# Feed-forward blocks of a two-layer encoder in seven products for eight, in a hand-written order

## The chip, the core and the metric

One core of a Trainium2 chip runs the whole program. The metric is the device time of one execution in microseconds. Engines: PE (TensorE) multiplies, DVE (VectorE), ACT (ScalarE) and POOL (GpSimd) work elementwise, SP issues the transfers.

## The reference, cut to what matters

1024 tokens of 1024 features go through two layers. Each adds a mixer's output and then that of a feed-forward block (SwiGLU with 2816 hidden features) to the residual h; the change is in the second.

```python
u = rms_norm(h, g_ffn[layer])
h = h + swiglu(u, w_gate[layer], w_up[layer], w_down[layer])

def swiglu(u, w_gate, w_up, w_down):
    return (jax.nn.silu(u @ w_gate) * (u @ w_up)) @ w_down
```

The inputs are float32. A product is made as three matmuls of fp32r operands: each operand x is split into a rounded part hi and a rest lo = x - hi, and hi*hi + hi*lo + lo*hi is summed in PSUM (`mm3`, lines 158 to 162).

## The kernel before

Activations stand transposed: features on the 128 partitions, tokens in two halves (hf 0 and 1) of 512 columns. h is 8 x 2 tiles of 128x512.

Order of work: mixer 0 (`mixer0`), feed-forward 0, mixer 1 (`mixer1`), feed-forward 1. A mixer ends in its output projection (`out_half`, lines 296 to 312), 8 tiles of 24 matmuls for each half; the first half's is woven into the attention, the second half's stands alone. There each new tile of h goes through `feed` (lines 205 to 213): times the gain, split, squared and summed. The normalisation itself (`rstd`, lines 191 to 203: a matmul with ones, Ln and Exp on ACT, three instructions on DVE) is put on the products' results later.

The feed-forward (`ffn`, lines 314 to 363) goes by chunks of the 22 hidden tiles (`CHUNKS`). For each hidden tile it loads 128x1024 of w_gate and w_up, splits them (`weight`, lines 146 to 156: hi on ACT, lo on POOL), makes four results of 8 x 3 matmuls each, and then: times r (DVE, 331), Silu (ACT, 332), times r (POOL, 333), times the second result (DVE, 336), split (ACT and DVE). After a chunk, its part of w_down is multiplied and added to h (`add`, lines 344 to 348). The last chunk also feeds what comes next: `to_mixer1` (line 954) in layer 0, `to_out` and `finish` in layer 1.

A scheduler orders each engine's instructions from the program's order and their dependences. PSUM has two banks "mm", two pairs "z" and two banks "o". The heap "u" has 60 tiles of 128x512. All transfers go through SP's queue, which issues in order.

Of the kernel before, what the change touches and what calls it, by code (L numbers as in the profile page):

```python
# [9 lines left out]
F32 = mybir.dt.float32  # L10
# [10 lines left out]
CHUNKS = [[(0, 6), (6, 6), (12, 5), (17, 5)], [(0, 6), (6, 6), (12, 6), (18, 4)]]  # L21
# [12 lines left out]
FFN_TEMPS = {"h": (18, 512), "w": (3, 1024)}  # L34


class Stream:


    def __init__(self):  # L40
        self.h = [[], []]
        self.u = [([], []), ([], [])]
        self.acc = [None, None]
        self.r = [None, None]
        self.rc = [None, None]


class Trunk:
    def __init__(self, ctx, tc, a):
        self.tc, self.nc, self.a = tc, tc.nc, a  # L50
        self.n = 0
        pool = lambda name, bufs, **k: ctx.enter_context(tc.tile_pool(name=name, bufs=bufs, **k))
        self.cp = pool("consts", 1)
        self.wp = pool("weights", 1)
        self.hp = pool("heap", HEAP)
        self.lp = pool("loads", LOADS)
        self.sp = pool("small", 4)
        self.ps = pool("psum", 1, space=bass.MemoryType.PSUM)
        self.dp = pool("spill", 1, space=bass.MemoryType.DRAM)
        self.turn = self.wturn = 0  # L60
        self.pending = []
# [34 lines left out]
    def any_banks(self):  # L96
        self.turn += 1
        if self.turn % 3 == 0:
            return [self.out_bank(), self.out_bank()]
        t = self.banks()  # L100
        return [t[:, 0, :], t[:, 1, :]]

# [24 lines left out]


# [16 lines left out]

    def weight(self, src, n=1024, eng_hi="act", eng_lo="pool", into=None):
        self.wturn = (self.wturn + 1) % 3
        if "w" in self.temps and self.wturn == 0:
            raw, *parts = (self.tmp("w", dt, (P, 1024)) for dt in (F32, F32R, F32R)[:1 if into else 3])
        else:  # L150
            raw, *parts = (self.wp.tile([P, 1024], dt, tag=t, bufs=2, name=self.nm(t))
                           for t, dt in (("wr", F32), ("wh", F32R), ("wl", F32R))[:1 if into else 3])
        hi, lo = into or parts
        self.nc.sync.dma_start(raw[:, :n], src)
        self.split(raw[:, :n], hi[:, :n], lo[:, :n], eng_hi, eng_lo)
        return hi, lo

    def mm3(self, out, wh, wl, xh, xl, first, last):
        mm = self.nc.tensor.matmul
        mm(out, wh, xh, start=first, stop=False)  # L160
        mm(out, wh, xl, start=False, stop=False)  # L161
        mm(out, wl, xh, start=False, stop=last)  # L162

    def dense(self, out, w, x, ks, m=P):
        wh, wl = w
        for i, k in enumerate(ks):
            self.mm3(out, wh[:, k * m:(k + 1) * m], wl[:, k * m:(k + 1) * m], x[0][k], x[1][k],
                     i == 0, i == len(ks) - 1)
            yield 3 * MM_US
# [59 lines left out]

    def start(self, vts, proj):  # L230
# [8 lines left out]
        def token_values(hf, k):  # L239
            n = 8 * hf + k  # L240
            self.feed(s, hf, self.load(a["x"][hf, k]) if n else x0, G_MIX0 + k, "pool")
            if n < 2:
                qk[n] = self.weight(a["w_qkb"][n], eng_hi=("act", "dve")[n], eng_lo="dve",
                                    into=[self.tmp("a", F32R, (P, 1024)) for _ in range(2)])
# [4 lines left out]
            wh, wl = vw[k // 4]  # L249
            ks = slice(k % 4 * 256, k % 4 * 256 + 256)  # L250
            for r in range(4):
                ts = slice(r * P, (r + 1) * P)
                self.mm3(psv[hf][:, r // 2, r % 2 * 256:r % 2 * 256 + 256], s.u[hf][0][k][:, ts],
                         s.u[hf][1][k][:, ts], wh[:, ks], wl[:, ks], k == 0 and r % 2 == 0, k == KD - 1 and r % 2 == 1)

        def query_key(hf, k):
            if k == 0:
                psq[hf] = [self.bank(), self.bank()]
            ks = slice(k * P, (k + 1) * P)
            for i in range(2):  # L260
                self.mm3(psq[hf][i], qk[i][0][:, ks], qk[i][1][:, ks], s.u[hf][0][k], s.u[hf][1][k],
                         k == 0, k == KD - 1)
# [33 lines left out]
    def out_half(self, hf, w, parts, resid, goff, ks, s):  # L296

        nc = self.nc
        o = [x[0] for x in parts], [x[1] for x in parts]
        ahead = []  # L300
        for m in range(KD):
# [3 lines left out]
            wt = self.weight(w[m])  # L305
            ps = self.bank()
            yield from self.dense(ps, wt, o, ks)
            nc.vector.tensor_tensor(h, ps, x, ALU.add)
            s.h[hf].append(h)
            self.feed(s, hf, h, goff + m)  # L310
        if hf == 0:
            self.close(s, hf)

    def ffn(self, layer, s, parts, hold, done):

        nc, a = self.nc, self.a
        hs = s.h
        self.wturn = 0
        for ci, (f0, nf) in enumerate(CHUNKS[layer]):
            h1 = [([], []), ([], [])]  # L320
            for f in range(f0, f0 + nf):
                ws = [self.weight(a[n][layer, f]) for n in ("w_gate", "w_up")]
                ps = [self.any_banks(), self.any_banks()]
                sils = {}
                for hf, i in ((0, 0), (0, 1), (1, 0), (1, 1)) if f == 0 else ((0, 0), (1, 0), (0, 1), (1, 1)):
                    self.now(self.dense(ps[i][hf], ws[i], s.u[hf], range(KD)))
                    if s.r[1] is None:
                        self.close(s, 1)
                    if i == 0:
                        t = sils[hf] = self.unit()  # L330
                        nc.vector.tensor_tensor(t, ps[0][hf], s.r[hf], ALU.mult)  # L331
                        nc.scalar.activation(t, t, AF.Silu)  # L332
                        nc.gpsimd.tensor_tensor(t, t, s.r[hf], ALU.mult)  # L333
                        continue
                    t = sils[hf]
                    nc.vector.tensor_tensor(t, t, ps[1][hf], ALU.mult)  # L336
                    hi = self.unit(F32R) if f - f0 < nf - 3 else self.tmp("h", F32R)
                    lo = self.tmp("h", F32R)
                    self.split(t, hi, lo, "act", "dve")
                    h1[hf][0].append(hi)  # L340
                    h1[hf][1].append(lo)
            wsrc = lambda m: a["w_down"][layer, m, :, f0 * P:(f0 + nf) * P]

            def add(w, hf, m, cs=slice(0, HALF)):
                ps = self.bank()[:, 0:cs.stop - cs.start]
                x = [t[:, cs] for t in h1[hf][0]], [t[:, cs] for t in h1[hf][1]]
                self.now(self.dense(ps, w, x, range(nf)))
                nc.vector.tensor_tensor(hs[hf][m][:, cs], ps, hs[hf][m][:, cs], ALU.add)  # L348

            if ci < len(CHUNKS[layer]) - 1:  # L350
                for m in range(KD):
                    w = self.weight(wsrc(m), nf * P)
                    for hf in range(2):
                        add(w, hf, m)
                continue
            self.use_exp_ln()
            held = []
            for n, (hf, cs) in enumerate(parts):
                for m in range(KD):
                    while hold and len(held) < min(m + 3, KD):  # L360
                        held.append(self.weight(wsrc(len(held)), nf * P, into=[self.unit(F32R), self.unit(F32R)]))
                    add(held[m] if hold else self.weight(wsrc(m), nf * P), hf, m, cs)
                    done(n, m)
# [37 lines left out]
    def values(self, wsrc, s, kper, nk, ng, vts, hfs):  # L401
# [6 lines left out]
        for b0 in range(4 * hfs[0], 4 * hfs[-1] + 4, per):  # L408
            ps = self.bank()
            for b in range(per):  # L410
                hf, r = divmod(b0 + b, 4)
                ts = slice(r * P, (r + 1) * P)
                for k in range(nk):
                    wh, wl = ws[k // kper]
                    ks = slice((k % kper) * ncol, (k % kper + 1) * ncol)
                    self.mm3(ps[:, b * ncol:(b + 1) * ncol], u[hf][0][k][:, ts], u[hf][1][k][:, ts],
                             wh[:, ks], wl[:, ks], k == 0, k == nk - 1)
# [419 lines left out]
    def mixer0(self):  # L837
# [4 lines left out]
        half = lambda hf: self.out_half(hf, a["w_out0"], o_p[hf], lambda hf, m: a["x"][hf, m], G_FFN0, ks, out)  # L842
        with self.phase("mix0", MIX0_TEMPS):
# [53 lines left out]
            self.now(half(1))  # L897
        return out

    def mixer1(self, u, h_d):  # L900
# [3 lines left out]
        half = lambda hf: self.out_half(hf, a["w_out1"], o_p[hf], lambda hf, m: h_d[hf][m], G_FFN1,  # L904
                                        list(range(KD)), out)
        with self.phase("band", BAND_TEMPS):
# [37 lines left out]
            self.now(half(1))  # L944
        return out

    def run(self):
        nc, a = self.nc, self.a
        self.use_exp_ln()
        s = self.mixer0()  # L950
        h_d = self.spill("h_")
        nxt = Stream()

        def to_mixer1(hf, m):
            h = s.h[hf][m]
            self.feed(nxt, hf, h, G_MIX1 + m)
            nc.sync.dma_start(h_d[hf][m], h)
            if m == KD - 1:
                self.close(nxt, hf, columns=True)

        with self.phase("ffn0", FFN_TEMPS):
            self.ffn(0, s, [(hf, slice(0, HALF)) for hf in range(2)], False, to_mixer1)
        s = self.mixer1(nxt, h_d)
# [26 lines left out]
        with self.phase("ffn1", FFN_TEMPS):  # L990
            self.ffn(1, s, parts, True, to_out)
# [17 lines left out]
def _layout(i):  # L1009
# [40 lines left out]
    out["w_down"] = np.stack([_mtiles(i["w_down"][l]) for l in range(2)])  # L1050
# [38 lines left out]
```

## Time and profile before

| | |
|---|---|
| median of 3 runs | 2765.8 us (2762.65 to 2766.0) |
| the profiled execution | 2765.65 us |
| its span, first to last instruction | 2763.9 us |
| granted TensorE clock, mean | 0.994 |
| first feed-forward stage, about | 700 to 1410 us of the span |
| second feed-forward stage, about | 2010 us to the end |

In the profile a slice is a fortieth of the span (69 us), and each digit a busy share in tenths. A row of the timeline gives start, duration, engine, line, operation, out<-in, and in brackets how long the engine stood idle before it, and for whom. In a row of windows each engine has its busy microseconds and (x instructions). Matmul durations overlap (0.39 us each), so their spacing counts.

### The profile page before, as it was taken

Reading aid. Unit: us, or ns where it says so; the run is one execution under the profiler, and the core shown is the slowest. Engines: PE = TensorE matmul, PEld = TensorE weight load, DVE = VectorE, ACT = ScalarE, POOL = GpSimd, SP = SyncE. Lnnn points to the kernel's source line nnn. Section 1 sums busy time; section 2 is a strip of 40 time slices with the busy share of each in tenths; the row PEclk is TensorE's granted clock in tenths of the full one; section 3 lists DMA queues with packets and bytes.
Section 4 is the critical chain, followed back from the end, with each engine's and each line's share of the span. In section 5 each row is a group of like instructions: output and inputs, shape, how many; then the busy total and the mean of one; then the engine's idle time right before and its main releaser. Section 6 shows DMA issues by size and latency. Waiting matters only on the chain.

```text
span 2763.9 us, 31577 instructions
## 1 busy us (share of the span) xinstructions
PE 2694.1 (97%) x12502; PEld 2075.4 (75%) x12502; DVE 1359.1 (49%) x1899; ACT 936.0 (34%) x1419; POOL 967.4 (35%) x697
## 2 busy tenths in 40 slices
PE   7999989999999999999999999999999999999997
PEld 6766755567888888888887777766788888888886
DVE  6889787776321221222356666678742122122125
ACT  4766675454211111211243333334421111111114
POOL 3333225664332322323322334334433233233233
PEclk9999999999999999999999999999999999999999
DMA  4222100134111111111142222223411111111111
GB/s 134 54 62 65 37 15 24 45 115 130 59 39 56 49 39 57 40 52 54 50 147 68 80 69 80 79 73 109 149 62 38 54 54 37 56 51 38 58 39 69
DMA packets 69827, 178.49 MB, mean 65 GB/s; under 512 B 8368, under 2 KB 12336, under 8 KB 69680
## 3 DMA queue, kind: packets, MB, share of 16 engines
q1 hardware_dynamic: 69680, 176.48, 20.3%
q8 instruction: 98, 1.61, 0.2%
q14 instruction: 49, 0.40, 0.0%
HBM read 150.23 MB, written 15.73 MB: 60 GB/s over the span
## 4 chain that ended last, share of the span: by engine, by line
PE 80%; DVE 5%; issue 1%; ACT 1%; POOL 0%; DVEq 0%; ACTq 0%; POOLq 0%
PE mm L160 11%; PE mm L161 11%; PE mm L162 11%; PE z L160 8%; PE z L161 8%; PE z L162 8%; PE o L161 4%; PE o L162 4%; PE o L160 4%; PE o L435 4%; PE z L805 2%; PE z L779 1%; PE z L806 1%; PE z L724 1%; DVE f L697 1%
## 5 line engine op out<-in xcount | busy, mean ns | idle before, releaser
L140 POOL TENSOR_TENSOR wl<-wr,wh 128x1024 fp32r<-128x1024 f32 (+4 forms) x165 | 348.7, 2113 | 745.5 <-ACT wh L135 693.2
L160 PE MATMUL mm<-u,wh 128*128 128x512 f32 x970 | 389.3, 402 | 3.7 <-DVE u L137 2.0
L162 PE MATMUL mm<-u,wl 128*128 128x512 f32 x970 | 380.0, 392 | 0.1
L135 ACT CAST wh<-wr 128x1024 fp32r<-128x1024 f32 (+4 forms) x175 | 164.7, 941 | 598.2 <-PE mm L161 278.4
L161 PE MATMUL mm<-u,wh 128*128 128x512 f32 x768 | 301.7, 393 | 0.0
L160 PE MATMUL z<-u,wh 128*128 128x512 f32 x672 | 266.3, 398 | 0.0
L161 PE MATMUL z<-u,wh 128*128 128x512 f32 x672 | 262.5, 391 | 0.0
L162 PE MATMUL z<-u,wl 128*128 128x512 f32 x672 | 261.7, 389 | 0.0
L348 DVE TENSOR_TENSOR u<-mm,u 128x512 f32<-128x512 f32 (+1 forms) x136 | 89.6, 659 | 311.9 <-PE mm L162 311.4
L160 PEld LDWEIGHTS mm<-u,wh 128*128 128x128 f32 x970 | 182.4, 188 | 75.7 <-issue 32.9
L162 PEld LDWEIGHTS mm<-u,wl 128*128 128x128 f32 x970 | 182.3, 188 | 40.4 <-issue 2.9
L140 POOL TENSOR_TENSOR w<-w,w 128x1024 fp32r<-128x1024 f32 (+2 forms) x50 | 105.7, 2115 | 260.2 <-ACT w L135 260.2
L435 PE MATMUL o<-a,u 128*64 128x512 f32 (+3 forms) x768 | 174.1, 483 | 0.2 <-ACT a L808 0.2
L333 POOL TENSOR_TENSOR u<-u,u 128x512 f32<-128x512 f32 x88 | 114.5, 1302 | 159.5 <-ACT u L332 159.5
L336 DVE TENSOR_TENSOR u<-u,z 128x512 f32<-128x512 f32 x60 | 41.3, 689 | 262.3 <-PE z L162 223.1
L161 PEld LDWEIGHTS mm<-u,wh 128*128 128x128 f32 x768 | 144.7, 188 | 29.4 <-issue 4.6
L161 PE MATMUL mm<-h,wh 128*128 128x512 f32 x424 | 166.2, 392 | 0.0
L160 PEld LDWEIGHTS z<-u,wh 128*128 128x128 f32 x672 | 126.1, 188 | 39.2 <-DVE u L336 7.0
L676 POOL TENSOR_TENSOR b<-b,a 128x512 f32<-128x512 f32 (+3 forms) x80 | 108.1, 1352 | 117.0 <-ACT a L808 101.1
L162 PEld LDWEIGHTS z<-u,wl 128*128 128x128 f32 x672 | 126.2, 188 | 27.1
L331 DVE TENSOR_TENSOR u<-z,u 128x512 f32<-128x512 f32 x58 | 40.1, 692 | 214.4 <-PE z L162 214.4
L161 PEld LDWEIGHTS z<-u,wh 128*128 128x128 f32 x672 | 126.2, 188 | 25.5 <-issue 0.5
(225 smaller groups left out, 5990.5 us busy)
## 6 DMA issues: line engine op xcount, KB each, us to landing
wr<-in_w_out SPq DMA_DIRECT2D x32, 512.0 KB, 3.3
wr<-in_w_gate SPq DMA_DIRECT2D x31, 512.0 KB, 3.2
wr<-in_w_up SPq DMA_DIRECT2D x29, 512.0 KB, 3.2
wr<-in_w_down SPq DMA_DIRECT2D x27, 384.0 KB, 3.1
u<-u SPq DMA_DIRECT2D x80, 128.0 KB, 2.2
wr<-in_w_qk SPq DMA_DIRECT2D x18, 512.0 KB, 3.7
ld<-in_x SPq DMA_DIRECT2D x32, 256.0 KB, 2.9
w<-in_w_up SPq DMA_DIRECT2D x15, 512.0 KB, 3.2
```

The costliest lines, as they stand in the source:

```text
L135: self.nc.scalar.copy(hi, src)
L140: self.eng(eng).tensor_tensor(lo, src, hi.bitcast(F32), ALU.subtract)
L160: mm(out, wh, xh, start=first, stop=False)
L161: mm(out, wh, xl, start=False, stop=False)
L162: mm(out, wl, xh, start=False, stop=last)
L331: nc.vector.tensor_tensor(t, ps[0][hf], s.r[hf], ALU.mult)
L333: nc.gpsimd.tensor_tensor(t, t, s.r[hf], ALU.mult)
L336: nc.vector.tensor_tensor(t, t, ps[1][hf], ALU.mult)
L348: nc.vector.tensor_tensor(hs[hf][m][:, cs], ps, hs[hf][m][:, cs], ALU.add)
L435: self.nc.tensor.matmul(o[rh, cs], vt[j // 4][:, j % 4, rh], w[:, e, cs], start=first, stop=last)
L676: self.eng("dve" if dest[2] else "pool").tensor_tensor(st["esum"][:, :, cs], old[:, :, cs], ex[:, :, cs], ALU.add)
L805: mm(z[:, e, cs], ks[e][kh][0][:, bs], qs[e][hf][0][:, cs], start=True, stop=False)
```

## The change

Products of blocks are made in seven for eight, by the scheme of Strassen in Winograd's form. The hidden tiles go in 11 pairs. For a pair the weight is a 2x2 of blocks (two output tiles by two halves of the features), and the operand a 2x2 of blocks (two halves of the features by two halves of the tokens). Weight sums s1 to s4 and operand sums t1 to t4 replace plain blocks in some products; results add up in PSUM or in SBUF. One unit (`Seven`) takes the gate's and the up weight of a pair side by side (t = 0, 1): 14 products of 12 matmuls, in the order 1, 2, 5, 6, 3, 7, 4. Product 6 adds onto the bank of 1, then 7 and 4 as well; between them the partial sum is read out (`put`).

The hidden results and their sums t1 to t4 are written to DRAM, the sums already split, the plain ones not, by `hidden`. Behind the 11 units come three groups of 3, 3 and 3 pairs for w_down, each of two units with 14 products of 9 matmuls (`down`); their operands are loaded from DRAM as the products of the unit before end. The last 2 pairs go as before, plainly.

All work of the feed-forward up to that last group is pinned to the program's order on PE, DVE, ACT and POOL (`pinned`). Rounding (ACT) is put 4 products ahead of its use (`HI`), the low part (DVE) 3 (`LO`). Low parts of weights and operands are on DVE, none on POOL. The normalisation is applied before the products: `blocks0` for the first half of the tokens while the second half of the output projection runs (this now comes inside the feed-forward's loop, its weights' low parts on DVE), `blocks1` for the second half during the first products. To give `blocks1` time, products 1 and 2 of the second unit come ahead of product 5 of the first. h is kept in DRAM meanwhile. Weights everywhere are loaded and split in pieces of 512 columns, not 1024.

```diff
-CHUNKS = [[(0, 6), (6, 6), (12, 5), (17, 5)], [(0, 6), (6, 6), (12, 6), (18, 4)]]
+GROUPS = [3, 3, 3, 2]
+HI, LO = 4, 3
...
+class Seven:
+    ORDER = "1256374"
+    USES = {"1": ("11", "11"), "2": ("12", "21"), "5": ("s1", "t1"), "6": ("s2", "t2"), "3": ("s4", "22"),
+            "7": ("s3", "t3"), "4": ("22", "t4")}
...
+    def product(self, p, t):
...
+        self.ps = self.y[t] if p == "2" else self.z[t] if p in "53" else self.x[:, t, :]
+        for i, (xh, xl) in enumerate(xs):
+            wh, wl = w.at(i * P, P)
+            k.mm3(self.ps, wh, wl, xh, xl, p in "125" and i == 0, i == len(xs) - 1, p in "6743")
...
+    def parted(self, t, eng="dve"):
+        hi, lo = self.unit(F32R), self.unit(F32R)
+        self.split(t, hi, lo, "act", eng)
+        return hi, lo
...
+    def blocks1(self, s, goff):
+        tt, u, n, t2 = self.nc.vector.tensor_tensor, s.h, KD // 2, []
+        s.r[1] = self.rstd(s.acc[1], D)
+        yield
+        for k in range(n):
+            self.normal(s, 1, k, goff, s.r[1])
+            tt(u[0][k], u[1][k], u[0][k], ALU.subtract)
+            s.ops["t1"].append(self.parted(u[0][k]))
+            yield
...
+        for k in range(n):
+            tt(u[1][k], u[1][n + k], u[1][k], ALU.subtract)
+            s.ops["t3"].append(self.parted(u[1][k]))
+            yield
...
+        def put(p, t, ps):
+            if p in "156":
...
+                nc.scalar.copy(c, ps)
+                return
...
+            c = kept[{"2": "1", "3": "6", "7": "5"}[p], t]
+            tt(c, ps, c, ALU.add)
+            if t == 0:
+                nc.scalar.activation(c, c, AF.Silu)
+                gate[name] = c
+            else:
+                tt(c, c, gate[name], ALU.mult)
...
+            steps = [(sv, p, t) for sv in todo for p in Seven.ORDER for t in range(2)]
+            steps[4:18] = steps[14:18] + steps[4:14]
...
+            todo1 = self.blocks1(s, goff)
+            after[0].append(lambda: next(todo1))
+            for n, k in ((3, 1), (4, 1), (5, 1), (6, 1), (7, 2), (8, 2), (9, 2), (10, 2), (11, 2), (12, 2), (13, 2), (14, 2)):
+                at[n] += [lambda: next(todo1)] * k
+            def run(n):
+                if n >= 0:
+                    sv, p, t = steps[n]
+                    sv.product(p, t)
+                for f in at.pop(n, ()):
+                    f()
+                for f, d in ((Seven.hi, HI), (Seven.lo, LO)):
+                    if 0 <= n + d < len(steps):
+                        w, q, e = steps[n + d]
+                        f(w, q, e)
+                if n >= 0:
+                    sv.put(p, t, sv.ps)
+                for f in after.pop(n, ()):
+                    f()
...
+            for k, _ in enumerate(rest):
+                if k % 4 == 2:
+                    next(b0, None)
...
+                    for k, x in ((w["7", t] - HI - 1, "11"), (w["3", t] - LO, "12"), (w["7", t] - LO, "21"),
+                                 (w["4", t] - LO, "22")):
+                        after[k].append(lambda x=x, nx=nx: nx.load(x))
```

VectorE's order where the first feed-forward's first products run. Before (z_5821 and z_5822 are the two results of the first hidden tile, u_5424 and u_5851 the roots of the two halves):

```order
L185 TENSOR_TENSOR u_5495<-u_5495,u_5786 128x512
L198 TENSOR_SCALAR u_5849<-o_5847 128x512
L331 TENSOR_TENSOR u_5858<-z_5821,u_5424 128x512
L200 TENSOR_TENSOR u_5849<-u_5849,u_5851 128x512
L201 TENSOR_TENSOR u_5849<-u_5849,u_5851 128x512
L202 SCALAR_TENSOR_TENSOR u_5851<-u_5849,u_5851 128x512
L336 TENSOR_TENSOR u_5858<-u_5858,z_5822 128x512
L140 TENSOR_TENSOR h_5888<-u_5858,u_5887 128x512
```

After, at the same place (all written through one helper, L74; o_6264 and o_6283 are product 2 of the first unit, u_5760 and u_5816 tiles of the second half of h, u_6237 its root, u_5143 and u_5187 tiles of the first half, wl and vl low parts of weights):

```order
L74 TENSOR_TENSOR ld_6231<-o_6264,ld_6231 128x512
L74 SCALAR_TENSOR_TENSOR u_5760<-u_5760,gains,u_6237 128x512
L74 TENSOR_TENSOR u_5143<-u_5760,u_5143 128x512
L74 TENSOR_TENSOR u_6299<-u_5143,u_6298 128x512
L74 TENSOR_TENSOR wl_6304<-e_6165,wh_6277 128x512
L74 TENSOR_TENSOR ld_6262<-o_6283,ld_6262 128x512
L74 TENSOR_TENSOR ld_6262<-ld_6262,ld_6231 128x512
L74 SCALAR_TENSOR_TENSOR u_5816<-u_5816,gains,u_6237 128x512
L74 TENSOR_TENSOR u_5187<-u_5816,u_5187 128x512
L74 TENSOR_TENSOR u_6325<-u_5187,u_6324 128x512
L74 TENSOR_TENSOR vl_6330<-e_6177,vh_6302 128x512
```

Between the sums of products stand normalising, subtracting and splitting blocks: u_6298 is ScalarE's rounding of u_5143, which is written one row earlier.

Some fifty rows on, where the last blocks (t4) are made and product 7 of the first unit (z_6212) is read out:

```order
L74 TENSOR_TENSOR u_5435<-u_5435,u_6406 128x512
L74 TENSOR_TENSOR u_6596<-u_5435,u_6595 128x512
L74 TENSOR_TENSOR wl_6601<-wr_6118,wh_6567 128x512
L74 TENSOR_TENSOR e_6541<-mm_6454,e_6541 128x512
L74 TENSOR_TENSOR e_6541<-e_6541,e_6509 128x512
L74 TENSOR_TENSOR s_6619<-vr_6573,e_6418 128x512
L74 TENSOR_TENSOR u_5480<-u_5480,u_6435 128x512
L74 TENSOR_TENSOR u_6623<-u_5480,u_6622 128x512
L74 TENSOR_TENSOR u_5541<-u_5541,u_6442 128x512
L74 TENSOR_TENSOR u_6628<-u_5541,u_6627 128x512
L74 TENSOR_TENSOR vl_6633<-vr_6132,vh_6599 128x512
L74 TENSOR_TENSOR e_6452<-z_6212,e_6452 128x512
```

The matmuls of product 4 add onto z_6212 and come behind that last row; nothing of this stood there before.

SP's queue in the second unit of the first group of w_down, from the unit's sixth product on (wr and vr are quarters of weights for the next unit, u and ld operands of the next group from DRAM); these are the 13th to 24th of a run of 24 loads:

```order
L94 DMA wr_10270<-in_w_down 128x384
L587 DMA u_10294<-f_3_t_5679 128x512
L587 DMA u_10296<-f_3_t_5680 128x512
L94 DMA vr_10292<-in_w_down 128x384
L587 DMA u_10298<-f_4_t_5690 128x512
L587 DMA u_10300<-f_4_t_5691 128x512
L587 DMA u_10302<-f_5_t_5701 128x512
L587 DMA u_10304<-f_5_t_5702 128x512
L182 DMA ld_10344<-f_3_220_5676 128x512
L94 DMA wr_10324<-in_w_down 128x384
L182 DMA ld_10360<-f_4_220_5687 128x512
L94 DMA vr_10342<-in_w_down 128x384
```

Before, this queue held only one weight load after the other in these stages; now operands stand between them.

More of the change, by code (lines that the diff above doesn't have):

```diff
@@ L45, in __init__, with at, __getattr__ @@
         self.rc = [None, None]
+        self.ops = {x: [] for x in ("11", "21", "22", "t1", "t2", "t3", "t4")}
+class Weight:
+    def __init__(self, parts, per=HALF):
+        self.parts, self.per = parts, per
+    def at(self, c, n):
+        hi, lo = self.parts[c // self.per]
+        cs = slice(c % self.per, c % self.per + n)
+        return hi[:, cs], lo[:, cs]
+class Pinned:
+    def __init__(self, tc, eng):
+        self.tc, self.eng = tc, eng
+    def __getattr__(self, name):
+        f = getattr(self.eng, name)
+        return lambda *a, **k: self.tc.keep_in_program_order(f(*a, **k))
@@ L228, in columns, with halves @@
         nc.vector.tensor_copy(s.rc[hf], ps[:, 0:4])
+    def halves(self, tiles):
+        return [tuple(t[:, c:c + HALF] for t in tiles) for c in (0, HALF)]
     def start(self, vts, proj):
@@ L309, in out_half @@
             s.h[hf].append(h)
[L310 to L314, printed above, removed]
-        nc, a = self.nc, self.a
[L317 to L363, printed above, removed]
@@ L896, in mixer0, with mixer1 @@
                 mla = nxt
-            self.now(half(1))
-        return out
-    def mixer1(self, u, h_d):
+        return out, half(1, 1)
+    def mixer1(self, u, h_d, h2_d):
         a = self.a
@@ L943, in mixer1 @@
                 proj, tq, tk = nxt, tqn, tkn
-            self.now(half(1))
-        return out
+        return out, half(1, 1)
     def run(self):
```

364 lines of the change are left out of this document (312 added, 52 removed).

## The prediction

> **What bounds the kernel now.** I read the page first, then the windows of the feed-forward stage, then the timelines of single engines.
>
> ```profile
> PE 2694.1 (97%) x12502; PEld 2075.4 (75%) x12502; DVE 1359.1 (49%) x1899; ACT 936.0 (34%) x1419; POOL 967.4 (35%) x697
> ...
> PE   7999989999999999999999999999999999999997
> ...
> DVE  6889787776321221222356666678742122122125
> ...
> PE 80%; DVE 5%; issue 1%; ACT 1%; POOL 0%; DVEq 0%; ACTq 0%; POOLq 0%
> ```
>
> TensorE is busy everywhere and holds 80% of the chain that ended last. VectorE is loaded in the mixers (slices 1 to 11 and 20 to 30), and at two tenths in the two feed-forward stages. These stages are where the change works, so I look at one.
>
> ```profile
> core 0: us, PE busy (x) PEld busy (x) DVE busy (x) ACT busy (x) POOL busy (x), PEclk, DMA share, GB/s
> 800.00:1300.00 500.00, 500.00 (x2188) 408.69 (x2187) 111.70 (x134) 82.70 (x109) 146.62 (x82) 1.00 0.16 49
> ...
> 1403.72 0.39 PE L160 MATMUL mm<-h,w 128*128 128x512 f32 x1
> ...
> 1405.08 0.39 PE L160 MATMUL mm<-u,wh 128*128 128x512 f32 x1
> ```
>
> There is no gap on TensorE in 500 us: the stage costs what its matmuls cost. From 1403.72 to 1405.08 stand six intervals, 1.36 us, so one matmul of 512 columns takes 0.2267 us. (500 us over 2188 records would give 0.2285; some records are missing, so I take the spacing.)
>
> **What the change removes on TensorE.** Per layer, before: 22 hidden tiles x 2 weights x 2 halves x 8 steps x 3 = 2112, and 8 x 2 x 22 x 3 = 1056 behind them, 3168 in all. After: 11 units of 14 products with 12 matmuls (1848), 6 units of 14 products with 9 (756), and the last group unchanged in kind, 8 x 2 x 4 x 3 = 192: 2796. (In layer 1 a part of the last group goes in 256 columns, the same number in both kernels.) That is 372 a layer, 744 in all, and 744 x 0.2267 = **168.7 us**, if TensorE stays the bound. A product of 12 then takes 2.72 us, one of 9 2.04 us.
>
> **Does VectorE keep up?** It gets the work: sums of weights, all low parts, and sums of products.
>
> ```profile
> 1000.75 0.69 DVE L336 TENSOR_TENSOR u<-u,z 128x512 f32<-128x512 f32 x1 [4.82 <-PE z L162]
> 1002.13 0.69 DVE L140 TENSOR_TENSOR h<-u,h 128x512 fp32r<-128x512 f32 x1 [0.69 <-ACT h L135]
> ...
> 1008.75 1.68 DVE L140 TENSOR_TENSOR h<-u,h 128x512 fp32r<-128x512 f32 x1 [0.69 <-ACT h L135]
> ...
> 1008.04 1.84 POOL L140 TENSOR_TENSOR w<-w,w 128x768 fp32r<-128x768 f32 x1 [8.21 <-ACT w L135]
> ...
> 655.78 0.69 DVE L696 SCALAR_TENSOR_TENSOR f<-z,f 128x512 f32<-128x512 f32 x1
> 656.38 0.68 DVE L201 TENSOR_TENSOR u<-u,u 128x512 f32<-128x512 f32 x1
> 656.98 0.69 DVE L697 SCALAR_TENSOR_TENSOR f<-f,f 128x512 f32<-128x512 f32 x1
> ...
> 706.72 0.69 DVE L201 TENSOR_TENSOR u<-u,u 128x512 f32<-128x512 f32 x1
> 707.45 0.69 DVE L202 SCALAR_TENSOR_TENSOR u<-u,u 128x512 f32<-128x512 f32 x1
> ```
>
> The same operation takes 0.69 us alone and 1.68 us beside one on GpSimd. Without GpSimd work I count 0.69. Queued without waits such instructions start 0.60 us apart (655.78, 656.38), one that needs the one before it 0.73 (706.72, 707.45). One that needs ScalarE's rounding of the one before waits 0.69 longer. A steady hidden unit has 40 VectorE instructions: 8 sums, 14 low parts of weights, 10 on the products' results, 8 on spilled operands. 40 x 0.69 = 27.6 us against 14 x 2.72 = 38.1 us. Two units behind them have 81 (44 on 384 columns), at most 81 x 0.69 = 55.9 us against 28 x 2.04 = 57.1 us. So in the steady units VectorE, with orders four steps ahead for ScalarE and three for VectorE, is hidden. At GpSimd's 1.68 it would not be.
>
> **The join from mixer to feed-forward is the main cost.** Blocks are now normalised ahead of the products, by VectorE: a multiplication, for three of the operands a subtraction, ScalarE's rounding, the low part. The order of VectorE shown above has each of these directly behind what it needs, so each exposes the 0.69.
> (a) While the second half of the output projection runs, each of its tiles holds 24 matmuls, 5.44 us. VectorE has per tile: the residual sum and the wait for ScalarE's square 1.38, the sum of squares 0.60, two low parts 1.20, and two blocks of normalise, wait and low part, 2 x 1.98. That is 7.14 us, 1.7 too much, for four tiles: 6.8 us, behind a chain of the root that fills the first tile. With two banks TensorE feels all but the first: I take 5.5 us.
> (b) Then the blocks of the second half. From the sum that reads o_6264 (third product of the first unit) to the sum that reads z_6212 (its product 7) stand 68 VectorE instructions. 24 belong to the units, about 0.62 each, 14.9 us. The rest are 8 blocks of three instructions, 0.73 + 0.69 + 0.69 + 0.60 = 2.7 each, 21.7 us; four low parts 2.4; 8 pairs of subtraction, wait, low part, 1.98 each, 15.8. Sum 54.8 us. Product 4 adds onto the bank that this sum reads, so it cannot start before. In between TensorE has 13 products, 35.4 us. VectorE starts 0.6 us late: 0.6 + 54.8 - 35.4 = 20.0 us. The matmul with ones (L195 below, 0.66 us) waits another 0.5 for the last square.
>
> So 26 us a join, **52 us** for two layers. Low end: if the rounding waits find cover, 24 x 0.69 = 17 us a join go, and 10 us a join stay, 20 in all. High end: every instruction at 0.69 instead of 0.60, on 68 of them 6 us, and 4 us more for ScalarE's longer waits: 72.
>
> **Smaller terms.**
>
> ```profile
> 650.00:652.00 2.00, 0.34 (x2) 0.15 (x2) 1.80 (x2) 0.00 (x0) 0.65 (x1) 1.00 0.15 23
> ...
> 1970.00:1980.00 10.00, 8.65 (x40) 5.57 (x39) 7.99 (x11) 4.62 (x7) 2.40 (x1) 1.00 0.26 79
> ```
>
> Before, the root of the first half stops TensorE where that half closes, 1.66 + 1.35 us. After, it is asked for inside the second half: -3 us (0 to -3.3).
>
> ```profile
> 1379.13 0.69 DVE L348 TENSOR_TENSOR u<-mm,u 128x512 f32<-128x512 f32 x1
> 1380.61 1.27 DVE L210 SCALAR_TENSOR_TENSOR u<-u,gains,u 128x512 fp32r<-128x512 f32 x1 [0.79 <-ACT u L209]
> 1381.81 0.68 DVE L185 TENSOR_TENSOR u<-u,u 128x512 f32<-128x512 f32 x1
> 1382.53 0.69 DVE L348 TENSOR_TENSOR u<-mm,u 128x512 f32<-128x512 f32 x1
> ```
>
> The last group of layer 0: VectorE's cycle is 3.40 us, just the 15 matmuls of a step. A step has 12 now, 2.72 us, and the cycle is 2.8 without and up to 3.3 with GpSimd's collision on L210. About 0.25 x 16 = +4 us (0 to 10).
>
> ```profile
> q1 hardware_dynamic: 69680, 176.48, 20.3%
> ...
> wr<-in_w_down SPq DMA_DIRECT2D x27, 384.0 KB, 3.1
> ```
>
> Transfers: 176.48 MB in 20.3% of 2763.9 us is 314 GB/s while all engines work. In the second unit of a group, the operands of the next group (33 loads of 0.262 MB) come among 8 of weights (0.197 MB). The queue's order above has the quarter wr_10324 as the 22nd load from the unit's sixth product on: 5.4 MB, 17.2 us, and some 2 us to land (3.1 for 384 KB, less 1.25 of transfer), 9.4 products later. The sum that needs it stands 8 products later: 2.8 us late, four times, **+11 us** (0, if weights' lead holds, to 25, if the queue is also held by spills before the first such unit). [...]
>
> ```profile
> 1407.46 1.05 PE L225 MATMUL o<-ones,u 1*128 1x1 f32 x8 [2.00 <-DVE u L202]
> ...
> 1409.42 0.63 PE L161 MATMUL mm<-h,wh 128*128 128x512 f32 x1
> 1409.84 0.63 PE L162 MATMUL mm<-h,wl 128*128 128x512 f32 x1
> ```
>
> Behind a stop of 2.0 us and eight tiny products matmuls stand 0.42 us apart, for eight of them: 1.6 us lost. The wait before product 4 is longer: +3 us for two joins (0 to 7). [...]
>
> ```profile
> L531 DVE TENSOR_TENSOR a<-a,z 128x1024 f32<-128x1024 f32 x24 | 29.2, 1215 | 0.2
> L195 PE MATMUL o<-u,ones 128*128 128x512 f32 x26 | 14.9, 657 | 5.4 <-DVE u L185 5.4
> ```
>
> In the mixers weights are split in halves of 512 columns, twice as many instructions, but 2 x 0.60 is no more than the 1.22 us of a whole one of 1024: nothing, within 5 us, as long as ScalarE, at 20 to 70% there, covers its additional starts.
>
> **Sum.** From the profiled execution's own 2765.65 us (median of the shown runs 2765.8, so the same): 2765.65 - 168.7 - 3 + 52 + 4 + 11 + 3 = **2664**.
>
> **Rivals.**
> 1. The joins are covered after all (ScalarE's answers come while other instructions run): 20 instead of 52, and 7 less for late weights, 2625. For it: the change sends two products of the second unit ahead of the blocks. Against: the order of VectorE is strict, and 0.69 stands in every such pair of the trace.
> 2. Slower: the transfer queue. SP issues in order, and spills wait there for VectorE and ScalarE ahead of loads of weights. If a unit's last quarter comes L too late, each of the 34 units waits L. It decides from (2765.65 - 2664)/34 = 3.0 us; at 4 us the time is 2800. Against: the share of transfers in the old stage is 0.16, and the steady hidden unit moves 19 tiles, 5 MB, 16 us at 314 GB/s in 38 us.
> 3. VectorE is the bound in the units too, at a mean of 1.2 us instead of 0.69 as beside GpSimd: 40 x 1.2 = 48 against 38.1 us, 10 us in 22 units and some 20 in 12: 3100 or so. Against: GpSimd has nothing to do there.
> 4. The change does not do what it says, because a change of bank costs: 476 products at 0.2 us, 95 us, 2759. Against: 3.40 us for 15 matmuls is 0.2267 each, bank changes included.
>
> **Chances.** Forecast 0.65, rival 1 0.20, rival 2 0.07, rival 3 0.03, rival 4 0.03, others 0.02. The ends: all low terms 2765.65 - 168.7 - 3.3 + 20 = 2614, all high 2765.65 - 168.7 + 72 + 10 + 25 + 7 = 2711. Both at once are unlikely; 2618 to 2711 takes in the first rival and leaves out the others, about 0.15. About 0.2% can be told from no change here: faster 0.87 (with a third of rival 4), same 0.03, slower 0.10.
>
> **What would show it.** The profile after should have 744 matmuls fewer; in the middle of the hidden stage a TensorE without gaps at 0.2267 and VectorE at about 70%; two stretches of 55 us behind the mixers with VectorE full and TensorE stopped some 20 us; low parts at 0.69. I am wrong if TensorE waits in the steady units (for which engine or transfer, the waits would say), or if the joins show no stop.

## The result, and the profile after

| | before | after |
|---|---|---|
| time, median (range) | 2765.9 us (2762.7 to 2766.9) | 2835.4 us (2829.6 to 2837.5) |
| after / before | | 1.025, interval 1.0232 to 1.0268 |
| span of the profiled execution | 2763.9 us | 2827.9 us |
| start of the first feed-forward's first product | 697.6 us | 700.4 us |
| last root of the first feed-forward read out | 1438.8 us | 1469.3 us |
| start of the second feed-forward's first product | 2024.5 us | 2052.8 us |

The kernel is 2.5% slower, where 3.7% faster was forecast: 171 us between the two. The table says where to look. The stretches of the mixers (from the start to the first product, and from 1438.8 to 2024.5, now from 1469.3 to 2052.8) moved by +3 and -2 us. The feed-forward stages got longer, by 28 and 36 us; the forecast had them shorter by some 50 each.

The page of the kernel after, at the lines that were shown of before:

```profile
PE 2577.5 (91%) x11758; PEld 1935.5 (68%) x11758; DVE 1915.5 (68%) x3072; ACT 1168.1 (41%) x2028; POOL 519.3 (18%) x489
...
PE   8999989999799899988999999999969999998887
...
DVE  6888788666756556566666777777675556566665
...
PE 63%; DVE 15%; ACT 4%; issue 3%; DMA 2%; DVEq 0%; SPq 0%; ACTq 0%
```

The 744 matmuls are gone (12502 to 11758), and TensorE's busy time fell by 117 us. But its share fell from 97 to 91%, and its share of the chain from 80 to 63%: the time went into gaps. VectorE stands at five to seven tenths in the feed-forward slices, where about 70% was forecast for the hidden stage, and nowhere near full. So no engine has too much work; the work comes at the wrong time.

The waits of TensorE in 350 us in the middle of the hidden stage, 800 to 1150 us (who waits for whom, us in total, times, the longest):

```profile
PE z L74 <- DVE e L74: 14.1, 17, 0.9
PE z L74 <- ACT e L74: 10.9, 16, 0.7
PE z L74 <- ACT ld L74: 5.4, 8, 0.7
```

41 waits, all of products into z, all under 1 us, all for tiles of results (e and ld). Not one is for a weight (w, v) or a transfer. One unit in the timeline of the same kernel, those rows of TensorE that waited, and beside them the rows that read a z out:

```profile
858.34 0.58 ACT L74 COPY ld<-z 128x512 f32<-128x512 f32 x1 [4.80 <-PE z L74]
...
901.58 0.58 ACT L74 COPY ld<-z 128x512 f32<-128x512 f32 x1 [4.79 <-PE z L74]
902.22 0.73 PE L74 MATMUL z<-u,vh 128*128 128x512 f32 x2 [0.68 <-ACT ld L74]
...
918.87 0.58 ACT L74 COPY e<-z 128x512 f32<-128x512 f32 x1 [1.61 <-PE z L74]
...
919.51 0.73 PE L74 MATMUL z<-u,vh 128*128 128x512 f32 x2 [0.68 <-ACT e L74]
...
930.73 0.69 DVE L74 TENSOR_TENSOR e<-z,e 128x512 f32<-128x512 f32 x1 [0.63 <-PE z L74]
...
931.47 0.73 PE L74 MATMUL z<-u,vh 128*128 128x512 f32 x2 [0.78 <-DVE e L74]
...
934.54 0.69 DVE L74 TENSOR_TENSOR e<-z,e 128x512 f32<-128x512 f32 x1 [2.53 <-PE z L74]
935.38 0.70 PE L74 MATMUL z<-u,wh 128*128 128x512 f32 x2 [0.88 <-DVE e L74]
...
938.39 0.60 ACT L74 ACTIVATE e<-z 128x512 f32<-128x512 f32 x1 [5.28 <-PE z L74]
939.04 0.73 PE L74 MATMUL z<-u,vh 128*128 128x512 f32 x2 [0.69 <-ACT e L74]
```

Each wait is the same picture. A product ends; ScalarE or VectorE reads its result out of z (0.58 to 0.69 us); the next product starts right behind that reading. But the next product goes into the other half of the pair: vh stands for the second half (w_up), the reading just ahead of it for the first (w_gate). At 935.38 it is the other way: product 4 of the first half starts behind the reading of product 7's second half. Five such places in a unit of 14 products: 1, 6 and 7 (second half each), and both halves of product 4. From the reading at 858.34 to the same one at 901.58 are 43.24 us, where 14 x 2.72 = 38.1 was forecast: 5.2 us a unit, and for 34 units 176 us, about what is missing.

The program says the same. Where the second half of product 1 begins, TensorE's list for the third unit has one wait, and the signal that it waits for is the one that ScalarE gives at its copy of the first half:

TensorE's list:

```
L74 MATMUL z_6929<-u_5956,wl_6884 128x512
L74 MATMUL z_6929<-u_5863,vh_6882 128x512 [waits Activation_49]
```

ScalarE's list, where that signal is given:

```
L74 COPY ld_6949<-z_6929 128x512 [waits PE_49]
```

The rounding of the weight, vh_6882, stands five rows ahead of this copy, so it is not what the product waits for. The first matmuls of the other four products wait in the same way for the instruction that reads the other half. The two halves are banks of their own, but one tile by name (z_6929), and the tile is what is tracked. That is the theory tested first.

### The profile page after: what moved, and what is told of

It reads as the page before. It is cut to its first block, busy times and chain, and to the rows that moved or that the text cites. A ratio compares the mean times of both kernels' runs of the same rounds, so it can differ in the third digit from the quotient of the medians.

```text
span 2827.9 us, 33576 instructions
## 1 busy us (share of the span) xinstructions
PE 2577.5 (91%) x11758; PEld 1935.5 (68%) x11758; DVE 1915.5 (68%) x3072; ACT 1168.1 (41%) x2028; POOL 519.3 (18%) x489
## 4 chain that ended last, share of the span: by engine, by line
PE 63%; DVE 15%; ACT 4%; issue 3%; DMA 2%; DVEq 0%; SPq 0%; ACTq 0%
PE z L74 23%; PE mm L74 10%; PE o L74 6%; PE mm L268 5%; PE mm L269 5%; PE mm L270 5%; DVE u L74 4%; PE o L791 3%; ACT u L74 2%; DVE f L1053 1%; PE z L1161 1%; DVE e L74 1%; DMA ld<-f 1%; PE z L1135 1%; PE z L1162 1%
## 5 line engine op out<-in xcount | busy, mean ns | idle before, releaser
L74 PE MATMUL z<-u,vh 128*128 128x512 f32 x992 | 333.3, 418 | 137.3 <-DVE u L74 47.2
L74 PE MATMUL z<-u,wh 128*128 128x512 f32 x992 | 310.5, 394 | 32.6 <-DVE e L74 19.3
L74 PEld LDWEIGHTS z<-u,vh 128*128 128x128 f32 x992 | 183.3, 196 | 226.7 <-ACT e L74 54.3
L268 PE MATMUL mm<-u,wh 128*128 128x512 f32 x720 | 291.4, 405 | 3.3 <-issue 1.9
L243 POOL TENSOR_TENSOR wl<-wr,wh 128x512 fp32r<-128x512 f32 (+2 forms) x95 | 121.5, 1286 | 910.2 <-PE z L74 756.0
L269 PE MATMUL mm<-u,wh 128*128 128x512 f32 x720 | 284.3, 395 | 1.4 <-DVE u L243 1.4
L74 PEld LDWEIGHTS z<-u,wh 128*128 128x128 f32 x992 | 183.7, 188 | 85.4 <-issue 29.5
L74 PE MATMUL mm<-u,wh 128*128 128x512 f32 x720 | 223.4, 391 | 6.2 <-ACT wh L74 6.2
L74 PE MATMUL z<-u,vl 128*128 128x512 f32 x496 | 199.8, 403 | 0.0
L74 PE MATMUL z<-u,wl 128*128 128x512 f32 x496 | 193.4, 390 | 0.0
L268 PEld LDWEIGHTS mm<-u,wh 128*128 128x128 f32 x720 | 135.5, 188 | 63.1 <-issue 34.1
L74 PEld LDWEIGHTS mm<-u,wh 128*128 128x128 f32 x720 | 134.7, 188 | 37.2 <-ACT wh L74 8.8
L269 PEld LDWEIGHTS mm<-u,wh 128*128 128x128 f32 x720 | 135.6, 188 | 32.7 <-issue 8.3
L74 PE MATMUL mm<-u,vh 128*128 128x512 f32 x496 | 152.7, 389 | 0.0
L74 DVE TENSOR_TENSOR u<-z,u 128x512 f32<-128x512 f32 x96 | 66.2, 690 | 119.9 <-PE z L74 119.9
L74 PE MATMUL mm<-u,wl 128*128 128x512 f32 x360 | 140.8, 391 | 0.8 <-DVE wl L74 0.5
L74 DVE TENSOR_TENSOR e<-z,e 128x512 f32<-128x512 f32 x66 | 45.6, 691 | 136.3 <-PE z L74 136.2
```

The costliest lines, as they stand in the source:

```text
L74: return lambda *a, **k: self.tc.keep_in_program_order(f(*a, **k))
L243: self.eng(eng).tensor_tensor(lo, src, hi.bitcast(F32), ALU.subtract)
L268: mm(out, wh, xh, start=first, stop=False, skip_group_check=onto)
L269: mm(out, wh, xl, start=False, stop=False, skip_group_check=onto)
```

## The experiments

**1. Halves from different pairs.**

```diff
-            self.x = k.banks()
+            self.x = k.pairs_x[k.units_made % 2]
+            k.units_made += 1
...
-        self.ps = ... else self.x[:, t, :]
+        self.ps = ... else self.x[t]
...
+        za, zb = self.banks(), self.banks()
+        self.pairs_x = [[za[:, e, :], zb[:, e, :]] for e in range(2)]
```

> Edit: the two halves of a unit's x no longer lie in one pair of banks under one name; each half is taken from another pair, and the pairs are kept for the whole feed-forward. Products, their order, the sums and the transfers stay. Theory (the pair is tracked as one tile, so a product into one half waits until the other half has been read out; five such waits of 0.84 to 1.19 us in each unit, 4.8 to 5.1 us a unit, 34 units): they go, TensorE stands without gaps in the steady hidden units (period 43.2 to about 38.3 us), and the time falls by 34 x 4.8 = 163 us to about 2670, between 2650 and 2700. Rival A (a change of bank costs TensorE itself 0.9 us): as many changes of bank remain, so the time stays at about 2835. Rival B (VectorE, or late transfers in each unit, stand behind the waits): other waits take the place of the removed ones, and less than half of it is gained, 2755 or more.

Measured: 2651.3 us (2650.1 to 2652.3), 0.9588 of before (0.9573 to 0.9602), so 184 us less than the change and at the lower end of what the theory said. The page, and the window that was shown above:

```profile
PE 2532.3 (96%) x11758; PEld 1946.3 (74%) x11758; DVE 1913.6 (72%) x3072; ACT 1169.3 (44%) x2028; POOL 520.9 (20%) x489
```

```profile
core 0: us, PE busy (x) PEld busy (x) DVE busy (x) ACT busy (x) POOL busy (x), PEclk, DMA share, GB/s
800.00:1150.00 350.00, 350.00 (x1546) 289.91 (x1545) 233.81 (x374) 146.54 (x267) 0.00 (x0) 1.00 0.45 154
```

No gap in 350 us, and 1546 matmuls where the change had 1359 and 319.64 us busy. The copies of product 1 out of z in the timeline of this run:

```profile
841.22 0.59 ACT L74 COPY ld<-z 128x512 f32<-128x512 f32 x1 [3.48 <-PE z L74]
843.93 0.59 ACT L74 COPY ld<-z 128x512 f32<-128x512 f32 x1 [1.61 <-PE z L74]
...
879.29 0.59 ACT L74 COPY ld<-z 128x512 f32<-128x512 f32 x1 [3.48 <-PE z L74]
```

A unit has two of them, for the two halves, now 2.71 us apart, with no gap between the products. From the first of one unit to the first of the next are 38.07 us, 14 products of 2.719. Counted over the whole trace, what lies between two matmul starts beyond 0.2267 us (where they are over 0.25 us apart) is 263 us, where the change has 439: the 176 us again. Both rivals fall: as many changes of bank remain, and nothing stands behind the waits, neither VectorE nor a transfer.

**2. The pairs kept, but both halves from one.** The first experiment changed two things: which banks go together, and that the pairs are no longer taken and given back in each unit. This one undoes only the first.

```diff
-        self.pairs_x = [[za[:, e, :], zb[:, e, :]] for e in range(2)]
+        self.pairs_x = [[z[:, t, :] for t in range(2)] for z in (za, zb)]
```

> Edit: as in the run with halves from different pairs, two pairs are kept for the whole feed-forward and units take them in turn; but both halves of a unit's x lie in one pair again. It differs from that run only in which of the same four banks a half lies in. Theory (the pair is tracked as one tile): the five waits of each unit are back, about 2835, between 2820 and 2850. Rival (what went was the taking and giving back of the pair in each unit, not the tracking): it stays at about 2651.

Measured: 2834.2 us (2831.1 to 2838.1), 1.025 of before. The waits from 800 to 1150 us:

```profile
PE z L74 <- DVE e L74: 14.1, 17, 0.9
PE z L74 <- ACT e L74: 10.9, 16, 0.7
PE z L74 <- ACT ld L74: 5.4, 8, 0.7
```

They are the change's own, to the digit. The same four banks, products, sums and order, and one line decides over 183 us: whether the half that is written shares its tile with the half that is being read.

**3. The pair as in the change, another order of products.** From the third unit on a product into another bank stands between two halves.

```diff
+            mixed = [("1", 0), ("2", 0), ("1", 1), ("2", 1), ("5", 0), ("6", 0), ("5", 1), ("6", 1),
+                     ("3", 0), ("7", 0), ("3", 1), ("7", 1), ("4", 0), ("4", 1)]
+            for k, sv in enumerate(todo):
+                if k > 1:
+                    steps[14 * k:14 * k + 14] = [(sv, p, t) for p, t in mixed]
```

> Edit: the pair of banks stays as in the changed kernel, but from the third unit on the 14 products of a unit stand in another order, 1 2 1 2 5 6 5 6 3 7 3 7 4 4 with the halves in turn, so that a product into another bank stands between the two halves of products 1, 6 and 7. Theory (waits for the read of the other half): three of five waits find cover, about 2.7 to 2.9 us a unit; product 4, whose halves still stand together behind product 7, keeps about 2 us. 32 units x 2.8 = 90 us less, about 2745, between 2725 and 2775. Rival A (a change of bank costs TensorE 0.9 us): the order has more changes of bank, 14 of 14 for some 9, so it gets slower by about 32 x 4 x 0.9 = 115 us, 2950. Rival B (VectorE or transfers stand behind the waits): no change, 2835.

Measured: 2745.9 us (2740.3 to 2750.4), 0.9927 of before (0.991 to 0.9944), 90 us less than the change. The waits from 800 to 1150 us:

```profile
PE z L74 <- DVE e L74: 8.7, 10, 0.9
PE z L74 <- ACT e L74: 6.2, 9, 0.7
```

Some two waits a unit are left of five, those around product 4, as the order has it. Neither TensorE's work nor its operands changed, only what stands between a reading and the next writing of a pair. More changes of bank made it faster, which a cost of the change itself can't do.

**4. The join: low parts behind the next block.**

```diff
-        self.split(t, hi, lo, "act", eng)
+        self.round_to("act", hi, t)
+        self.low()
+        self.owed = (lo, t, hi)
...
+    def low(self):
+        if self.owed:
+            self.rest("dve", *self.owed)
+        self.owed = None
```

> Edit, in the join from mixer to feed-forward alone: a block's low part is issued on VectorE behind the instructions of the next block, so that ScalarE's rounding runs beside them. The units stay as in the changed kernel. Theory (the join is held by VectorE's strict order, with ScalarE's 0.69 us exposed some 24 times): 24 x 0.69 = 16.6 us a join at most; about 10 to 16 us a join are gained, 20 to 32 us in all, about 2810. Rival (the join is held by something else, the root's chain, the clock or transfers): less than 6 us, 2830 to 2835.

Measured: 2805.9 us (2801.5 to 2807.5), 1.0144 of before (1.0129 to 1.0159): 29.5 us less than the change. The waits of TensorE from 660 to 800 us, first of the change, then of this run:

```profile
PE z L74 <- DVE e L74: 10.2, 2, 9.3
PE z L74 <- ACT e L74: 4.5, 3, 3.1
PE z L74 <- ACT ld L74: 3.6, 1, 3.6
PE mm L74 <- ACT wh L74: 3.3, 3, 1.1
...
```

```profile
PE z L74 <- DVE e L74: 7.8, 4, 5.3
PE z L74 <- ACT e L74: 5.2, 4, 3.2
PE z L74 <- ACT ld L74: 2.3, 1, 2.3
PE z L74 <- DVE u L74: 1.2, 2, 1.0
...
```

The longest wait, for VectorE's sum out of product 7's first half, falls from 9.3 to 5.3 us. With both halves in one pair it stands before product 7's second half (a row z<-u,vh at 767.90 us of the change), one product ahead of product 4. The three waits of 1.1 us in the second half of the output projection (mm for wh) are gone. So some 15 us of each join came from VectorE's strict order, as forecast; what is left of it is not taken apart here.

**5. Both together.**

> Both edits together: halves of x from different pairs of banks, and low parts issued behind the next block. Theory: the gains are in different places and add up, about 2670 - 26 = 2645, between 2620 and 2680, and 4 to 5% faster than the kernel before the change (2766). Rival: with the units' waits gone, VectorE's backlog from the join is met earlier by product 4, or the transfers are late (the term of 11 us in the prediction grows): the sum is less than half additive, 2690 or more.

Measured: 2614.7 us (2613.3 to 2618.9), 0.9458 of before (0.9444 to 0.9472): 36.6 us less than with the halves apart alone. The gains add up, and a little more; the time is 5 us below the range that was expected. The waits from 660 to 800 us:

```profile
PE z L74 <- DVE e L74: 4.7, 1, 4.7
PE z L74 <- DVE u L74: 3.3, 4, 1.0
PE o L74 <- DVE u L74: 0.8, 1, 0.8
```

8.8 us of waits are left. All lines of this view give 25.4 for the change, some two units' own waits among these, and 20.5 for the run with halves apart alone.

**6. Two waits in the second units.** With the halves apart TensorE still stops before product 4 in the second unit of a group. The timeline of the run with both edits there:

```profile
1179.20 0.62 ACT L74 CAST u<-ld 128x512 fp32r<-128x512 f32 x1 [5.89 <-PE z L74]
...
1179.85 0.69 DVE L74 TENSOR_TENSOR u<-ld,u 128x512 fp32r<-128x512 f32 x1 [3.81 <-ACT u L74]
...
1180.93 0.68 DVE L74 TENSOR_TENSOR u<-z,u 128x512 f32<-128x512 f32 x1
...
1181.76 0.70 PE L74 MATMUL z<-u,wh 128*128 128x512 f32 x2 [2.37 <-DVE u L74]
```

Read upwards: product 4 waits for VectorE's sum out of z; the sum was queued behind the low part of an operand of the next group; and that waited 3.81 us for ScalarE's rounding. For the rounding this row names TensorE's matmuls into z (5.89 us), and the expectation below goes by it. The trace says otherwise. In the program the rounding waits for a matmul of product 6 and for the load of its operand. That matmul ended at about 1170 us; the load was issued at 1172.72 us and landed at 1179.12, 0.08 us ahead of the rounding. Ahead of the next such stop, that at 1241.04 us, the row itself names the load:

```profile
1238.48 0.62 ACT L74 CAST u<-ld 128x512 fp32r<-128x512 f32 x1 [5.28 <-DMA ld<-f]
```

In experiment 1, too, the rounding ahead of each of the four such stops starts 0.08 us behind the landing of its operand. So a transfer is late, as the prediction thought, but that of an operand, not of a quarter of the weights. The edit issues rounding and low part two products later:

```diff
-        at[n + 3].append(hi)
-        at[n + 4].append(lo)
+        at[n + 5].append(hi)
+        at[n + 6].append(lo)
```

> Edit, on top of halves apart and low parts behind the next block: of the operands that are spilled unsplit and split when they come back, the rounding on ScalarE and the low part on VectorE are issued two products later. Theory (in the second unit of a group ScalarE's rounding waits for a block that product 7 still reads, VectorE's low part waits for the rounding, and the sum that product 4 needs stands behind it; two such waits of 1.9 to 2.4 us in each layer): up to 4 x 2.1 = 8 us gained, about 2607. Rival of the prediction (what is late there is a quarter of the weights behind the operand loads in the transfer queue): the wait stays or grows by what is queued later, 2612 or more.

Measured: 2609.2 us (2604.7 to 2610.7), 0.9433 of before (0.9419 to 0.9447), where both edits alone had 0.9444 to 0.9472. The intervals touch, so the time alone settles little; the waits do. From 1150 to 1260 us, first without, then with the edit:

```profile
PE z L74 <- DVE u L74: 4.2, 2, 2.4
```

```profile
PE z L74 <- DVE u L74: 1.0, 2, 0.8
```

With the edit the rounding still starts right behind its load (landed at 1182.40 us, rounding at 1182.43), but product 4's sum now stands ahead of the low part in VectorE's order. So it is this order that cost the time; the transfer itself came no earlier. The rival, a late quarter of the weights, falls, since the waits shrank. This is the fastest version: 5.7% under before, 8% under the change.

**7 and 8. More work for VectorE.** On top of experiment 5, in the hidden units alone.

```diff
+        for _ in range(2 if n == HALF else 1):
             self.k.rest("dve", t[:, :n], self.raw[x][:, :n], self.parts[x][0][:, :n])
```

> Edit, on top of halves apart and low parts behind the next block: in the hidden units alone each low part of a weight is computed twice into the same place, 14 more VectorE instructions of 0.60 us in each of 22 units (8.4 us a unit, 308 instructions). Step of the prediction under test (VectorE is hidden behind TensorE with some 10 us to spare in a unit): the work is 40 x 0.69 + 8.4 = 36.0 of 38.1 us, so it stays hidden but in the two first units of a layer, where VectorE is behind already: 2 x 8 to 2 x 17 us more, 2631 to 2650. Rival (VectorE sets the time of the units): 22 x 8.4 = 185 us more, 2800.

> Edit: the same with three times, 28 more VectorE instructions a unit, 16.8 us. VectorE then has 68 instructions of at least 0.60 us, 41 us and more with its waits, against 38.1 of TensorE: the units become VectorE's. 22 x (3 to 6.5) + 2 x 17 = 100 to 177 us more than 2615, 2715 to 2790. If VectorE had more to spare than I think (waits that overlap with the added work), under 2690.

Measured: 2643.5 us with twice (2641.1 to 2646.2, 28.8 more than experiment 5), 2810.4 with three times (2807.5 to 2811.8, 196 more). The windows from 800 to 1150 us, of the one and of the other:

```profile
800.00:1150.00 350.00, 349.86 (x1544) 289.47 (x1544) 315.77 (x498) 146.91 (x268) 0.00 (x0) 1.00 0.46 154
```

```profile
800.00:1150.00 350.00, 316.84 (x1298) 251.49 (x1297) 339.78 (x528) 118.26 (x215) 0.00 (x0) 0.95 0.33 111
```

With 14 instructions more a unit, VectorE is at 90% and TensorE still has no gap: almost all of the 28.8 us falls in the joins (what lies there between matmul starts beyond 0.2267 us is about 26 us in each, and 13 to 14 without the added work). With 28 more VectorE is at 97%, and TensorE waits. So the room was there, between 8.4 and 16.8 us a unit, and the forecast's 10 fits. The expectation for three times (2715 to 2790) was 20 us short; it had not counted the clock, which this window has at 0.95, and that may be the rest.

## Why the prediction was wrong

The step that failed is in the first term: "744 x 0.2267 = 168.7 us, if TensorE stays the bound. A product of 12 then takes 2.72 us". The condition was then examined for the amount of VectorE's work and for transfers, and never for the banks that products are written to. It holds for the work (experiments 7 and 8), not for the places: in 34 units TensorE lost 5.2 us each, 176 us together, at waits for the other half of the pair that it was about to write. Waits of TensorE in the steady units were the sign that the prediction itself had named for being wrong.

Rival 4 came nearest, since it priced a change of bank, and was put away with "3.40 us for 15 matmuls is 0.2267 each, bank changes included". Those rows are of the last group, where each product goes into a tile of one bank (u<-mm in VectorE's rows). They say nothing on two products in a row into two halves of one tile. And its mechanism would have been another: not each change of bank costs, but five in a unit, in which the tile is the same.

With the pairs apart, the rest of the forecast can be read off. The first experiment is the change as the prediction took it to be, and 2651 us stand against 2664. With the values measured, the sum comes to about 2662; the other 11 us were not taken apart. These values are sums of what lies between two matmul starts of that run's timeline beyond 0.2267 us, where it is over 0.25 us.

| term | forecast | measured with halves apart |
|---|---|---|
| product of 12 matmuls | 2.72 us | 2.719 us (38.07 / 14) |
| (a) output projection, second half, per layer | 5.5 us | 5.1 and 4.6 us |
| (b) wait for product 4, ones, clock, per layer | 22 us | 24 and 26 us |
| last group of layer 0 | +4 us | below 1 us |
| late weights | 4 x 2.8 = 11 us | 4 waits of 1.8 to 2.1 us, 7.8 in all, behind a late operand |

- **The join** was right in mechanism and nearly in size. Only its place was off: of the 24 us in layer 0, 10.3 stand before product 4, where all 20 of (b) were put; the rest stands already at products of the second unit, which wait for ScalarE and VectorE, and behind most of these stops matmuls start 0.43 us apart. Experiment 4 took away 29.5 of the 2 x 17 us that the low end counted on. So rival 1 (joins covered) is false for the change, and nearly true after an edit of some ten lines: 13 to 14 us a join, for its 10.
- **Late weights**: the size was near, the queue right, the tile wrong. No product waited for a weight's transfer. What landed late was an operand, and the sum that product 4 needs stood behind it (experiment 6). Two figures of the sum were off: its 22 loads are 5.3 MB, not 5.4, and in this stretch the queue moved 381 to 397 GB/s (rows at the end), more than the 314 of the sum.
- **The last group**: VectorE's cycle was thought to be 2.8 to 3.3 us, for 2.72 of TensorE. The same operation in two cycles of the run with halves apart:

```profile
1362.32 0.75 DVE L317 SCALAR_TENSOR_TENSOR u<-u,gains,u 128x512 fp32r<-128x512 f32 x1 [0.19 <-ACT u L316]
...
1365.07 0.75 DVE L317 SCALAR_TENSOR_TENSOR u<-u,gains,u 128x512 fp32r<-128x512 f32 x1 [0.19 <-ACT u L316]
```

The cycle is 2.75 us, and the operation takes 0.75 us, where it took 1.27 in the trace of before.

- **Rival 2** (transfers late in every unit) and **rival 3** (VectorE) did not come: with the halves apart TensorE has no wait at all in the steady hidden units, and VectorE's instructions start 0.60 us apart as forecast. Rival 3 has its point: it begins between 14 and 28 more instructions a unit.

The sign of it was in the program before any run. In TensorE's list each of the five products begins with a wait on ScalarE or VectorE. It looks like a wait for the product's own weights, which many products have there; only the signal, followed back to the instruction that gives it, tells the two apart.

## What to carry to other kernels

When an order is written out by hand, ask of each two products in a row not only which bank they write, but which tile: in this program a wait is set for the tile, and two banks under one name are one. Then either part the names, or put a product into another tile between a reading and the next writing. And a row that stands for "no cost" must have the same neighbours as the place that it is to speak for. Where a trace names an engine as the end of a wait, look whether a transfer landed just then; the engine named may have been done long before, some 9 us in experiment 6.

## What the runs showed of the hardware beside

- The 41 stops of 0.67 to 0.88 us in the window of the change cost TensorE no clock:

```profile
800.00:1150.00 350.00, 319.64 (x1359) 251.55 (x1358) 205.11 (x327) 125.38 (x229) 0.00 (x0) 1.00 0.35 119
```

The granted clock is 1.00. Longer stops did cost it, but not each: in the run with halves apart two stops, of 1.71 and 1.90 us, ended at 1197.85 and 1257.16 us, and only the second was followed by half the clock. It was granted from 1257.32 us for 3.41 us, and the next time from 1967.29 us, 709.97 us or 208 times 3.413 us later. In the trace of the change half the clock is granted 14 times, for 3.41, 6.83 or 10.24 us (the last time up to the end of the trace), and its starts lie whole multiples of 3.413 us apart, so I count in steps of 3.41 us. The first two rows are the step that holds the first stop and the step behind it; the last two are the same for the second stop:

```profile
1195.88:1199.29 3.41, 1.70 (x8) 1.24 (x7) 3.29 (x6) 1.68 (x5) 0.00 (x0) 1.00 1.06 394
1199.29:1202.70 3.41, 3.41 (x16) 2.82 (x15) 1.77 (x4) 1.51 (x3) 0.00 (x0) 1.00 1.06 381
...
1253.91:1257.32 3.41, 1.51 (x7) 0.96 (x7) 2.07 (x4) 2.27 (x5) 0.00 (x0) 1.00 1.06 397
1257.32:1260.73 3.41, 3.41 (x9) 2.63 (x9) 1.23 (x3) 0.39 (x1) 0.00 (x0) 0.50 1.06 384
```

TensorE was idle for 50% of the first stop's step and for 56% of the second's. In the trace of the change, from 12 us on, there are 12 steps of full clock in which it was idle for over 55%, and all 12 were followed by half the clock; of the 552 in which it was idle for less than half, 2 were. In the trace of before it was 4 of 4, and 1 of 422.

- In experiment 1 TensorE wrote one bank while ScalarE read another, and neither was slower: the copies took 0.59 us, where they took 0.58 to 0.59 in the change, and a unit took 14 x 2.719 us, where 12 matmuls at 0.2267 are 2.720. Whether the chip itself would need a wait between the two banks of one pair was not tried.
- VectorE at 90% did not slow ScalarE or TensorE (experiment 7): TensorE was busy for 349.86 of 350 us, and ScalarE for 146.91 us with 268 instructions, 0.55 us each. Without the added work (experiment 5) these are 350.00 us, and 144.40 us with 264, 0.55 as well.
